# A recurrent and an attention layer on one core: the second half's attention input turned by transposing transfers

## The chip, the core and the metric

One core of one Trainium2 chip runs the whole program. Its engines are TensorE (PE in the profile; its weight loads are shown as PEld), VectorE (DVE), ScalarE (ACT), GpSimd (POOL) and SyncE (SP), which here only issues transfers. The metric is device time in microseconds (us) of one execution; lower is better.

## What is computed

Two layers on 256 tokens of width 1024, in fp32. Each layer is a feed-forward block, a mixer, and a second feed-forward block. The first layer's mixer is a gated linear recurrence, the second's is attention over keys and values that were computed from the first layer's output. The change lies at the entry to the second layer's attention and inside it. Cut to that, the reference is:

```python
f = swiglu(rms_norm(h, ffn1_pre_g[1]), ffn1_w_gate[1], ffn1_w_up[1], ffn1_w_down[1])
h = h + 0.5 * rms_norm(f, ffn1_post_g[1])
hn = rms_norm(h, mix_pre_g[1])
m = forgetting_attention(hn, attn_w_q[0], attn_w_o[0], k, v, c)
h = h + rms_norm(m, mix_post_g[1])

def forgetting_attention(xq, w_q, w_o, k, v, c):        # 16 heads of 64, blocks of 128 queries
    q = heads(xq @ w_q) * 64 ** -0.5
    for blk in range(2):
        logits = q[blk] @ k[:end].T + c[blk] - c[:end]  # end = 128, then 256; causal mask
        outs.append(softmax(logits) @ v[:end])
    return concat(outs) @ w_o
```

## The kernel before

**Tiles and halves.** The 256 tokens are two halves of 128 rows, t = 0 and t = 1. The residual `h[t]` is held with tokens in partitions. A product with a weight matrix needs its input turned, features in partitions; that turned input is the pair of tiles `xhi` and `xlo` with eight blocks k = 0 to 7 of 128 features each. Precision comes from a split: every weight and every input is written as an upper part (`hi`, a copy by ScalarE, L173 for weights) and the rest (`lo`, a difference by VectorE, L177), and a product is three matmuls: upper by upper, lower by upper, upper by lower.

**Units and slots.** The weights come in units of 512 KB (two blocks k by 512 columns for the q projection). A unit is loaded into one of 5 raw buffers by a transfer on SP's queue and split into one of 9 pairs of buffers. A slot is the work of one half on one unit, six large matmuls here (L454, L455, L458). `slot(t, i)` writes a slot's matmuls and ends with `tick()`. `prepare_next`, called by `tick`, loads and splits the next unit, as long as a unit of 9 places earlier is done in both halves; for the last four of W_o's eight units there is one more bound: unit i is not split before the first half has come to unit i - `near`, and `near = 3`.

**What sets the order.** TensorE's list is fixed by hand: it executes in the order in which the code was written. `defer(n, fn)` puts work off by n ticks, that is, by n slots. On the other engines a scheduler sets the order, in which work in `high_priority()` goes first and what is under `keep_in_program_order` keeps the order of writing. Each engine works through its list in that order, and an instruction that waits holds all behind it. The lists of SP and GpSimd include the transfers that they issue.

**The entry to attention.** `enter` ends a feed-forward block: it adds the normed output to `h[t]` (L298, L311) and puts off the making of the next input by `wait` = 3 slots. For attention, `inputs` does for each half: eight transposes on TensorE into two accumulators of tag `gt` (L226), a product with the gain on VectorE (L234), the upper part on ScalarE (L235), the rest on VectorE (L240). `stat` takes the sum of squares (L205) and two small GpSimd instructions (L198, L200) make the norm's factor from it, which is applied to q later. Elsewhere in the kernel the blocks k = 4 to 7 go another way (`by_transfer`): GpSimd copies the numbers into two planes of 16 bits (`planes`, L212), a transfer on SP's queue turns them (`swap`, L216), GpSimd puts the planes together (`join`, L220), and `turned_to_x` makes product, upper part and rest (L258, L259, L240).

**Attention.** For each half there are eight slots of q (two groups of 512 columns) and eight of W_o. When a group of q is complete, `heads_T` copies it to `htok` on VectorE (L1044). For t = 0 four transposes turn it (L1057, two slots later, copied to `qT` by ScalarE, L1059); for t = 1 the way over planes and a transfer is taken. Between the slots stand the small products of attention: `l` logits (L1194; then on VectorE the reduction with the bias, L1203, and on ScalarE eight exponentials, L1210), `n` the norming (L1217), `t` four transposes of probabilities (L1223, copied by ScalarE, L1225), and `v` the values (L1237). The string `ATT_ORDER` says in which order: a digit is a slot of that half, `l0` the next logits of the first half, and so on. The values gather in an accumulator of tag `mm` (four of these exist, two of each of the tags `gt` and `tr`):

```python
if hds[0] % 8 == 0:
    box["po"] = mmbank()
```

At the stage's begin `att_rows` loads the bias of the second half (2 MB) with a transfer on GpSimd's queue (L1038).

## Time and profile before

| what | value |
|---|---|
| median of three runs | 964.89 us (964.70 to 964.91) |
| profiled execution | 965.18 us, of which the span is 963.5 us |
| TensorE busy | 954.8 us, 99% |
| VectorE busy | 646.0 us, 67% |
| ScalarE busy | 527.5 us, 55% |
| GpSimd busy | 236.5 us, 25% |
| granted clock of TensorE | 0.999 |
| transfers | 199.84 MB, mean 207 GB/s |
| attention stage | from about 709 to 783 us of the span |

A row of the trace in order of time shows start, duration, engine, line, operation, `out<-in`, partitions by elements and type, and a count where several equal instructions are taken together; a bracket at its end gives the idle time before it and what ended that. Matmuls overlap their neighbours at start and end, so a difference of starts says what one costs, and not the duration. SPq and POOLq are the transfers that SP and GpSimd issue.

### The profile page before, as it was taken

To read this page: it belongs to the slowest core of one execution; us is meant where nothing else is said; L and a number is where in the kernel's file an instruction comes from. 1 tells how busy PE (TensorE), PEld (TensorE's weight loads), DVE (VectorE), ACT (ScalarE), POOL (GpSimd) and SP (SyncE) were. 2 spreads that over 40 slices of the span, in tenths; PEclk is the share of its full clock that TensorE was granted. 3 is DMA by queue.
4 is the path that set the end of the run, shared out by engine and by line. 5 is a ranking of instruction groups with operands and counts; after the bars stand their busy time and mean duration, and the time that the engine had idled before them with its cause. 6 is when DMAs were issued, how large, how long until landed. Compare 5 with 4: busy or idle time off the path is not lost.

```text
span 963.5 us, 12847 instructions
## 1 busy us (share of the span) xinstructions
PE 954.8 (99%) x4559; PEld 789.6 (82%) x4559; DVE 646.0 (67%) x845; ACT 527.5 (55%) x750; POOL 236.5 (25%) x229
## 2 busy tenths in 40 slices
PE   9999999999999999999999999999999999999997
PEld 6888888898878888888898888888887788888885
DVE  6758774578997756664686566665488876666642
ACT  7446454568986555444565445444366865444431
POOL 2812230130003323230023623224022133232200
PEclk9999999999999999999999999999999999999999
DMA  8788996485338687676559979879763478777731
GB/s 283 227 229 252 250 291 196 143 222 166 128 110 244 203 238 215 201 245 193 138 158 313 249 223 262 223 190 289 227 255 102 121 210 260 208 225 234 217 110 44
DMA packets 153158, 199.84 MB, mean 207 GB/s; under 512 B 71390, under 2 KB 90182, under 8 KB 152966
## 3 DMA queue, kind: packets, MB, share of 16 engines
q1 hardware_dynamic: 150406, 192.11, 67.4%
q0 software_dynamic: 2080, 6.38, 2.3%
q8 instruction: 36, 0.59, 0.2%
q10 hardware_dynamic: 608, 0.53, 0.2%
q14 instruction: 28, 0.23, 0.1%
HBM read 182.19 MB, written 3.16 MB: 192 GB/s over the span
## 4 chain that ended last, share of the span: by engine, by line
PE 95%; DVE 2%; ACT 1%; issue 1%; POOL 0%; DMA 0%; POOLq 0%; DVEq 0%; ACTq 0%
PE mm L454 16%; PE mm L455 16%; PE mm L458 16%; PE mm L183 13%; PE mm L185 13%; PE mm L184 13%; PE gt L824 2%; PE mm L1340 1%; PE mm L190 1%; PE mm L191 1%; PE mm L192 1%; ACT pe L1210 1%; PE gt L226 1%; PE tr L127 0%; DVE wlo L177 0%
## 5 line engine op out<-in xcount | busy, mean ns | idle before, releaser
L177 DVE TENSOR_TENSOR wlo<-raw,whi 128x1024 fp32r<-128x1024 f32 (+5 forms) x329 | 423.0, 1293 | 213.9 <-ACT whi L173 212.4
L173 ACT ACTIVATE whi<-raw 128x1024 fp32r<-128x1024 f32 (+5 forms) x329 | 341.6, 1045 | 295.8 <-PE mm L458 107.2
L454 PE MATMUL mm<-whi,xhi 128*128 128x512 f32 x656 | 256.7, 391 | 0.0
L455 PE MATMUL mm<-wlo,xhi 128*128 128x512 f32 x656 | 255.5, 389 | 0.0
L458 PE MATMUL mm<-whi,xlo 128*128 128x512 f32 x656 | 202.2, 389 | 0.0
L454 PEld LDWEIGHTS mm<-whi,xhi 128*128 128x128 f32 x656 | 123.2, 188 | 25.9 <-issue 0.7
L458 PEld LDWEIGHTS mm<-whi,xlo 128*128 128x128 f32 x656 | 123.1, 188 | 26.0 <-DVE xlo L240 0.2
L455 PEld LDWEIGHTS mm<-wlo,xhi 128*128 128x128 f32 x656 | 123.2, 188 | 25.3 <-DVE wlo L177 0.3
L183 PE MATMUL mm<-whi,hhi 128*128 128x512 f32 x352 | 137.2, 390 | 0.0
L185 PE MATMUL mm<-whi,hlo 128*128 128x512 f32 x352 | 137.0, 389 | 0.0
L184 PE MATMUL mm<-wlo,hhi 128*128 128x512 f32 x352 | 137.0, 389 | 0.0
L569 POOL COPY pl<-prod 128x1024 uint16<-128x1024 uint16 (+1 forms) x48 | 67.7, 1410 | 168.9 <-DMA prod<-pl 168.9
L556 POOL COPY pl<-prod 128x1024 uint16<-128x1024 uint16 (+1 forms) x48 | 70.1, 1460 | 141.8 <-DVE prod L553 74.4
L185 PEld LDWEIGHTS mm<-whi,hlo 128*128 128x128 f32 x352 | 66.1, 188 | 13.7
L183 PEld LDWEIGHTS mm<-whi,hhi 128*128 128x128 f32 x352 | 66.1, 188 | 13.7
L184 PEld LDWEIGHTS mm<-wlo,hhi 128*128 128x128 f32 x352 | 66.1, 188 | 13.6
L198 POOL TENSOR_SCALAR nv<-ss 128x1 f32<-128x1 f32 x22 | 11.4, 517 | 252.8 <-ACT junk L205 252.8
L553 DVE SCALAR_TENSOR_TENSOR prod<-mm,rstd,sil 128x512 f32<-128x512 f32 (+1 forms) x48 | 33.7, 703 | 29.1 <-PE mm L458 24.8
L544 ACT ACTIVATE sil<-mm,rstd 128x512 f32<-128x512 f32 (+1 forms) x48 | 31.1, 650 | 32.4 <-PE mm L458 24.8
L575 DVE TENSOR_TENSOR hlo<-pl,hhi 128x512 fp32r<-128x512 f32 (+1 forms) x48 | 41.2, 858 | 3.6 <-ACT hhi L574 3.6
L183 PE MATMUL mm<-whi,xhi 128*128 128x512 f32 (+1 forms) x112 | 42.8, 382 | 0.0
L185 PE MATMUL mm<-whi,xlo 128*128 128x512 f32 (+1 forms) x112 | 42.5, 379 | 0.0
(235 smaller groups left out, 1067.8 us busy)
## 6 DMA issues: line engine op xcount, KB each, us to landing
raw<-in_ffn_w_down_dram SPq DMA_DIRECT2D x88, 512.0 KB
raw<-in_ffn_w_up_dram SPq DMA_DIRECT2D x80, 512.0 KB
raw<-in_ffn_w_gate_dram SPq DMA_DIRECT2D x78, 512.0 KB
raw<-in_rg_w_in_dram SPq DMA_DIRECT2D x10, 504.0 KB
raw<-in_rg_w_out_dram SPq DMA_DIRECT2D x10, 504.0 KB
raw<-in_ffn_w_gate_dram SPq DMA_DIRECT2D x19, 256.0 KB
raw<-in_ffn_w_up_dram SPq DMA_DIRECT2D x16, 256.0 KB
raw<-in_rg_w_in_dram SPq DMA_DIRECT2D x8, 512.0 KB
```

Of the source, the lines that this page charges most:

```text
L173: up = nc.scalar.activation(hi[:parts, c:c + m], rawv[:, c:c + m], AF.Copy)
L177: nc.vector.tensor_tensor(lo[:parts, c:c + m], rawv[:, c:c + m], hi[:parts, c:c + m].bitcast(F32), ALU.subtract)
L183: nc.tensor.matmul(ps, xh, wh, start=first, stop=False)
L184: nc.tensor.matmul(ps, xh, wl, start=False, stop=False)
L185: nc.tensor.matmul(ps, xl, wh, start=False, stop=last)
L454: nc.tensor.matmul(ps, get_x(t, k)[0], u.hi[:, c], start=k == 0, stop=False)
L455: nc.tensor.matmul(ps, get_x(t, k)[0], u.lo[:, c], start=False, stop=False)
L458: nc.tensor.matmul(ps, get_x(t, k)[1], u.hi[:, c], start=False, stop=k == nk - 1)
L553: nc.vector.scalar_tensor_tensor(pr[:, :nn], ps, rs[t][:, 0:1], s, ALU.mult, ALU.mult)
L556: nc.gpsimd.tensor_copy(halves.rearrange("p (h f) -> p h f", h=2), pr[:, :nn].bitcast(U16).rearrange("p (f h) -> p h f", h=2))
L569: nc.gpsimd.tensor_copy(halves.rearrange("p (f h) -> p h f", h=2), turned.rearrange("p (h a) b -> p h (a b)", h=2))
L575: keep(nc.vector.tensor_tensor(lv, x, hv.bitcast(F32), ALU.subtract))
```

## The change

It has five parts.

1. For one place, the second half's input in front of attention (`whole`: the block before was a feed-forward block, there is one destination, and t = 1), all eight blocks k are now turned by transfers. `enter` copies both halves of `h[1]` to planes right behind the update of h. Three slots later `whole_inputs` issues the two transposing transfers, takes the sum of squares, and lets GpSimd join the planes. `turned_to_x`, which got an argument n for the group of blocks, follows for k = 0 to 3 after three more slots and for k = 4 to 7 after four. The eight transposes on TensorE, and the products, upper parts and rests that `inputs` made, are no longer there.
2. The load of the second half's bias is put off by seven slots.
3. `near` is 5 rather than 3, so the last four units of W_o may each be split two units earlier.
4. The second accumulator of the second half's values comes from tag `gt` rather than `mm`.
5. `ATT_ORDER` is another list. It has the same slots and the same small products; more of the latter stand beside each other.

```diff
-    def turned_to_x(v, dests, more):
+    def turned_to_x(v, dests, more, n=1):
...
-                g = gT[:, gi + 4:gi + 8].unsqueeze(2).to_broadcast([P, 4, P])
+                g = gT[:, gi + 4 * n:gi + 4 * n + 4].unsqueeze(2).to_broadcast([P, 4, P])
...
-                tc.keep_in_program_order(nc.scalar.activation(xh[:, 4:, :], xs[i], AF.Copy))
+                tc.keep_in_program_order(nc.scalar.activation(xh[:, 4 * n:4 * n + 4, :], xs[i], AF.Copy))
             for xg, dest in zip(xs, dests):
-                x_lower(xg, dest, 1)
+                x_lower(xg, dest, n)
...
         by_transfer = (spare or t == 1) and not (half and (len(dests) == 1 or t == 0)) and not normed
+        whole = half and len(dests) == 1 and t == 1 and not normed
+        if whole:
+            with tc.high_priority():
+                hp = [hpool.tile([P, 512], F32, tag="t1", name=nm("hp"), bufs=2) for _ in range(2)]
+                for n in range(2):
+                    planes(hp[n].bitcast(U16), h[t][:, n * 512:(n + 1) * 512])
...
+        def whole_inputs():
+            ht = [pools["a"].tile([P, 512], F32, tag="pT", name=nm("ht"), bufs=4).bitcast(U16) for _ in range(2)]
+            with tc.high_priority():
+                for n in range(2):
+                    swap(ht[n], hp[n].bitcast(U16))
+            stat(t)
+            with tc.high_priority():
+                for n in range(2):
+                    join(hp[n].bitcast(U16).rearrange("p (f h) -> p h f", h=2), ht[n])
+            for n in range(2):
+                defer(3 + n, lambda n=n: turned_to_x(hp[n], dests, None, n))
...
-            defer(wait, inputs)
+            defer(wait, whole_inputs if whole else inputs)
...
-    near = 3
+    near = 5
...
-        tc.keep_in_program_order(nc.gpsimd.dma_start(att["bias1"], kv["bias1"]))
+        defer(7, lambda: tc.keep_in_program_order(nc.gpsimd.dma_start(att["bias1"], kv["bias1"])))
...
-                box["po"] = mmbank()
+                box["po"] = mmbank() if t == 0 or hds[0] == 0 else gtbank()
...
-    ATT_ORDER = ("0 0 0 0 0 0 0 l0 0 1 n0 l0 1 1 t0 n0 1 l0 v0 1 t0 n0 l0 1 v0 n0 1 t0 l1 1 v0 t0 n1 l1 0 v0 "
+    ATT_ORDER = ("0 0 0 0 0 0 0 l0 0 1 n0 l0 1 1 n0 1 t0 t0 l0 1 n0 l0 1 n0 1 v0 v0 t0 1 l1 v0 t0 n1 l1 0 v0 n1 l1 0 t1 "
...
```

Lines behind the change stand lower by up to 18 in the changed kernel: the exponentials are L1228 there, the copies to qT L1077, the q slots L472, L473 and L476. The next pieces are the engines' lists, where `x4` means four of that kind in a row, and numbers behind a name count tiles.

GpSimd's list where attention begins, first before, then in the changed kernel; h_75 is the second half's residual, hp the planes, ht what the transfer turned, and nv and rstd belong to the norm's factor.

```order
L198 TENSOR_SCALAR nv_6329<-ss_6320 128x1
L200 TENSOR_TENSOR rstd_6331<-nv_6329,mhalf 128x1
L1038 DMA bias_6347<-bias1d 128x4096
L198 TENSOR_SCALAR nv_6394<-ss_6391 128x1
L200 TENSOR_TENSOR rstd_6396<-nv_6394,mhalf 128x1
L212 COPY pl_6538<-htok_6536 128x1024
L220 COPY qT_6346<-htok_6536 128x2x512
```

```order
L198 TENSOR_SCALAR nv_6329<-ss_6320 128x1
L200 TENSOR_TENSOR rstd_6331<-nv_6329,mhalf 128x1
L212 COPY hp_6335<-h_75 128x1024
L212 COPY hp_6336<-h_75 128x1024
L198 TENSOR_SCALAR nv_6383<-ss_6380 128x1
L200 TENSOR_TENSOR rstd_6385<-nv_6383,mhalf 128x1
L220 COPY hp_6335<-ht_6376 128x2x512
L220 COPY hp_6336<-ht_6377 128x2x512
L1056 DMA bias_6351<-bias1d 128x4096
L212 COPY pl_6529<-htok_6527 128x1024
```

Four copies are new, two in front of the small instructions of the second sum of squares and two behind them, and the bias's load has gone from the third place to behind the four.

ScalarE's list from the second half's sum of squares (L205) to the end of the first logits' exponentials, before and then changed; pe are exponentials, mx the negated maxima that they read, whi a weight unit's upper part, here of W_o, and xg or hp the second half's input.

```order
L205 ACTIVATE junk_6392,ss_6391<-h_75 128x1024
L235 ACTIVATE xhi<-xg_6383 128x4x128
L235 ACTIVATE xhi<-xg_6386 128x4x128
L1059 ACTIVATE qT_6345<-tr_6419 128x512
L1210 ACTIVATE pe_6443,sm_6441<-pe_6443,mx_6442 128x128 x4
L1210 ACTIVATE pe_6455,sm_6441<-pe_6455,mx_6454 128x128 x2
L1059 ACTIVATE qT_6345<-tr_6495 128x512
L1210 ACTIVATE pe_6455,sm_6441<-pe_6455,mx_6454 128x128 x2
L173 ACTIVATE whi_6483<-raw_6481 128x1024
```

```order
L205 ACTIVATE junk_6381,ss_6380<-h_75 128x1024
L1077 ACTIVATE qT_6349<-tr_6410 128x512
L259 ACTIVATE xhi<-hp_6335 128x4x128
L173 ACTIVATE whi_6481<-raw_6479 128x1024
L1228 ACTIVATE pe_6437,sm_6435<-pe_6437,mx_6436 128x128 x3
L1077 ACTIVATE qT_6349<-tr_6493 128x512
L1228 ACTIVATE pe_6437,sm_6435<-pe_6437,mx_6436 128x128
L1228 ACTIVATE pe_6449,sm_6435<-pe_6449,mx_6448 128x128 x4
L259 ACTIVATE xhi<-hp_6336 128x4x128
L173 ACTIVATE whi_6503<-raw_6501 128x1024
```

The two upper parts of the input stood together ahead of the first copy to qT; now the first stands behind that copy, and the second behind the last of the eight exponentials. The unit's upper part, which stood behind them all, is ahead of the exponentials.

VectorE's list in the same logits' reductions, before and changed; htok is the second group of q of the first half, and `ISA` is a reduction or the read of its result.

```order
L1203 ISA pe_6455,mx_6454<-gt_6432,bias_2952 128x128
L1203 ISA mx_6454 128x1
L1044 TENSOR_SCALAR htok_6472<-mm_6406,rstd_6270 128x512
L1208 TENSOR_TENSOR mx_6442<-mx_6442,cq_2947 128x4
L1203 ISA pe_6455,mx_6454<-gt_6431,bias_2952 128x128
L1203 ISA mx_6454 128x1
```

```order
L1221 ISA pe_6449,mx_6448<-gt_6426,bias_2952 128x128
L1221 ISA mx_6448 128x1
L1062 TENSOR_SCALAR htok_6466<-mm_6397,rstd_6270 128x512
L258 TENSOR_TENSOR hp_6336<-hp_6336,gT 128x512
L1226 TENSOR_TENSOR mx_6436<-mx_6436,cq_2947 128x4
L1221 ISA pe_6449,mx_6448<-gt_6425,bias_2952 128x128
L1221 ISA mx_6448 128x1
```

The product of the second part of the input (L258) now stands there, ahead of the small sum that makes the first exponentials' maxima.

More of the change, by code (lines that the diff above doesn't have):

```diff
@@ L1268, in trunk_kernel @@
               lambda t: None, last=True)
-    ATT_ORDER = ("0 0 0 0 0 0 0 l0 0 1 n0 l0 1 1 t0 n0 1 l0 v0 1 t0 n0 l0 1 v0 n0 1 t0 l1 1 v0 t0 n1 l1 0 v0 "
-                 "n1 l1 t1 0 n1 l1 t1 0 n1 l1 v1 v1 t1 0 n1 l1 t1 0 n1 l1 v1 v1 t1 0 n1 l1 t1 0 n1 v1 v1 0 t1 1 "
-                 "t1 v1 1 v1 1 1 1 1 1 1")
+    ATT_ORDER = ("0 0 0 0 0 0 0 l0 0 1 n0 l0 1 1 n0 1 t0 t0 l0 1 n0 l0 1 n0 1 v0 v0 t0 1 l1 v0 t0 n1 l1 0 v0 n1 l1 0 t1 "
+                 "n1 l1 t1 0 n1 l1 v1 v1 t1 0 n1 l1 t1 0 n1 l1 v1 v1 t1 0 n1 l1 t1 0 n1 v1 v1 0 t1 1 t1 v1 1 v1 1 1 1 1 1 1")
     def half(t, i):
```

## The prediction

> **What bounds the kernel now.** I read the page's line of busy engines first, then the windows over attention, then TensorE's rows there in order of time, and last what stands before those rows on the other engines.
>
> The first view is the page's part 1, the next one the windows of 20 us over attention (span, then busy time and instructions of PE, PEld, DVE, ACT and POOL, the granted clock, the DMA share and GB/s).
>
> ```profile
> PE 954.8 (99%) x4559; PEld 789.6 (82%) x4559; DVE 646.0 (67%) x845; ACT 527.5 (55%) x750; POOL 236.5 (25%) x229
> ```
> ```profile
> 700.00:720.00 20.00, 20.00 (x100) 16.67 (x98) 17.87 (x23) 14.75 (x22) 5.12 (x9) 1.00 0.67 249
> 720.00:740.00 20.00, 19.76 (x128) 14.97 (x126) 14.83 (x63) 11.73 (x40) 3.57 (x2) 1.00 0.48 159
> 740.00:760.00 20.00, 20.00 (x147) 15.12 (x148) 18.47 (x58) 15.71 (x40) 2.41 (x2) 1.00 0.37 95
> ```
>
> TensorE is busy 99% of the span, at full clock, and in these windows all but 0.24 us of 60. So the change gains only work or waits that it takes off TensorE's list, and loses every microsecond that it makes TensorE wait. VectorE has 17.87 and 18.47 of 20 us taken in two of the three windows: what is put in its way there shows.
>
> TensorE's own rows, in order of time (start, duration, line, names):
>
> ```profile
> 713.35 1.03 PE L226 MATMUL gt<-ident,h 128*128 128x128 f32 x8
> 714.14 0.48 PE L454 MATMUL mm<-whi,xhi 128*128 128x512 f32 x1
> 714.45 0.40 PE L455 MATMUL mm<-wlo,xhi 128*128 128x512 f32 x1
> 718.32 0.60 PE L1057 MATMUL tr<-ident,htok 128*128 128x128 f32 x4
> 722.83 0.40 PE L454 MATMUL mm<-whi,xhi 128*128 128x512 f32 x1
> 724.21 0.39 PE L454 MATMUL mm<-whi,xhi 128*128 128x512 f32 x1
> 725.58 0.60 PE L1057 MATMUL tr<-ident,htok 128*128 128x128 f32 x4
> 725.93 0.48 PE L454 MATMUL mm<-whi,xhi 128*128 128x512 f32 x1
> ```
>
> Here is the clock of the place. A slot (six large matmuls) takes 1.38 us (722.83 to 724.21). At 713.35 the eight transposes of the second half's h; at 718.32 and 725.58 the turns of the first half's q; at 722.83 the second half's first slot, at 725.93 its third, the first that reads the input's k = 4 to 7. I follow the change to these two slots.
>
> **The change part by part.**
>
> *The transposes go.* 713.35 to 714.14 is 0.79, and the matmul after them takes 0.31 instead of 0.23: 0.87 off TensorE. The q turn could then start at 717.45 instead of 718.32.
>
> *What comes instead* is two copies to planes and two back on GpSimd, two transposing transfers on SP's queue, and on VectorE and ScalarE a product, a copy and a difference per half. The product and the split replace as many of before, but stand elsewhere in their queues. VectorE in the trace of before:
>
> ```profile
> 711.51 1.41 DVE L311 SCALAR_TENSOR_TENSOR h<-t,rstd,h 128x512 f32<-128x512 f32 x2
> 712.84 2.35 DVE L177 TENSOR_TENSOR wlo<-raw,whi 128x1024 fp32r<-128x1024 f32 x2
> 721.44 0.29 DVE L1203 CUSTOM_DVE_ANT_0 pe<-gt,bias 128x128 f32<-128x128 f32 x1 [3.19 <-PE gt L1194]
> 721.66 0.08 DVE L1203 DVE_READ_ACCUMULATOR2_ANT mx<- 128x1 f32 x1
> 723.03 0.75 DVE L1044 TENSOR_SCALAR htok<-mm,rstd 128x512 f32<-128x512 f32 x1 [0.16 <-PE mm L458]
> ```
> ```profile
> 789.81 0.69 DVE L258 TENSOR_TENSOR hp<-hp,gT 128x512 f32<-128x512 f32 x1 [3.26 <-POOL hp L220]
> ```
>
> And the same copies of GpSimd, once with VectorE quiet and once beside two splits:
>
> ```profile
> 741.04 1.04 POOL L212 COPY pl<-htok 128x1024 uint16<-128x1024 uint16 x1 [3.74 <-DVE mx L1208]
> ```
> ```profile
> 781.51 1.97 POOL L212 COPY hp<-h 128x1024 uint16<-128x1024 uint16 x1 [1.51 <-DVE h L311]
> 788.43 1.34 POOL L220 COPY hp<-ht 128x1024 uint16<-128x1024 uint16 x1 [3.14 <-DMA ht<-hp]
> ```
> ```profile
> 781.36 3.19 DVE L177 TENSOR_TENSOR wlo<-raw,whi 128x1024 fp32r<-128x1024 f32 x2
> ```
>
> Alone the copy to planes takes 1.04. At 781.51 it takes 1.97, and the two splits under it 3.19 instead of 2.35 (712.84): the copy waited for the first split, the second split for the copy. The Trainium skill (SBUF — State Buffer, "Who interferes with whom") says why: a VectorE instruction with two SBUF inputs and a GpSimd instruction that reads SBUF exclude each other for the whole instruction. It adds that one with at most one SBUF input does not take part. This trace agrees with the first by 1.97 against 1.04. By the rule the sum is the one below, without it that of the first rival.
>
> In the changed kernel the two copies fall on the two splits at 712.84. The first half of h is there at 712.2; the copy waits for the second update and runs 712.9 to 713.9, a split to 715.05, the second copy to 716.05, the other split to 717.2 (before: 715.19), the q tile in 0.7 to 717.9. TensorE wanted it at 717.45: **a new wait of 0.5**. The second half's first slot then comes at 722.83 - 718.32 + 717.95 = 722.46.
>
> The transfers, and what waits for them:
>
> ```profile
> 732.50 1.25 SPq L216 DMA_TRANSPOSE htok<-pl  x1
> 783.51 1.25 SPq L216 DMA_TRANSPOSE ht<-hp  x1
> ```
> ```profile
> 735.62 1.68 POOL L220 COPY qT<-htok 128x1024 uint16<-128x1024 uint16 x1 [3.15 <-DMA htok<-pl]
> ```
>
> From the issue to the copy back it was 3.12 (732.50 to 735.62) and 4.92 (783.51 to 788.43, with other loads in the queue). From 713.95 and 716.1 that is 717.1 and 719.2 at best. GpSimd has its two small rstd instructions behind the last split, to 718.0, so the copies back (1.34 each) run to 719.35 and 720.7. The product of the first part (0.69) meets the second copy back and ends at 721.35, its xhi at 722.05, its xlo at 722.75: in time for the slot at 722.46, whose xlo products come 0.9 later. Late landing moves this by 0.2 only, since the product then goes ahead of the second copy.
>
> *The second part is the one that costs.* On VectorE it stands in the middle of the first logits' reductions, on ScalarE behind all eight exponentials of those logits. From 722.75: six reductions at 0.22 (721.44 to 721.66), the other q tile (0.7), the product (0.65) and two small sums: the first maxima are ready at 725.45. ScalarE's rows of before give the rest:
>
> ```profile
> 724.29 0.39 ACT L1210 ACTIVATE pe<-pe,mx 128x128 f32<-128x128 f32 x1
> 724.67 0.39 ACT L1210 ACTIVATE pe<-pe,mx 128x128 f32<-128x128 f32 x1
> 726.22 0.60 ACT L1059 ACTIVATE qT<-tr 128x512 f32<-128x512 f32 x1
> 726.71 0.39 ACT L1210 ACTIVATE pe<-pe,mx 128x128 f32<-128x128 f32 x1
> 727.48 1.04 ACT L173 ACTIVATE whi<-raw 128x1024 fp32r<-128x1024 f32 x1
> 728.42 0.58 ACT L1225 ACTIVATE pT<-tr 128x512 f32<-128x512 f32 x1
> ```
> ```profile
> 776.80 0.64 ACT L259 ACTIVATE xhi<-qT 128x512 fp32r<-128x512 f32 x1 [0.25 <-DVE qT L258]
> ```
>
> An exponential with its sum takes 0.38, the copy to qT 0.49, a W_o upper part 0.94, xhi 0.64. ScalarE's W_o upper part now stands ahead of the exponentials and waits for the second half's first slot, whose weight buffer it takes: 722.46 + 1.38 + 0.2 = 724.05, so it is through at 725.0, before the maxima. Then 725.45 + 8 x 0.38 + 0.49 + 0.64 = 729.6, and about 0.1 for the semaphores and starts: 729.7. TensorE has done two slots and the q turn (0.36) at 722.46 + 2.76 + 0.36 = 725.58, and its next row is the third slot, which reads that part. **A wait of 4.1.** Nothing behind it can pass: TensorE's list is fixed.
>
> *Fewer stretches.* What a stretch of small products costs beside itself:
>
> ```profile
> 733.87 0.62 PE L458 MATMUL mm<-whi,xlo 128*128 128x512 f32 x2
> 734.42 0.66 PE L1237 MATMUL mm<-pT,v 128*64 128x128 f32 x8
> 735.01 0.50 PE L454 MATMUL mm<-whi,xhi 128*128 128x512 f32 x1
> 735.35 0.39 PE L455 MATMUL mm<-wlo,xhi 128*128 128x512 f32 x1
> ```
> ```profile
> 737.35 0.73 PEld L1194 LDWEIGHTS gt<-kT,qT 64*128 64x128 f32 x8 [0.48 <-POOL qT L220]
> ```
>
> After two matmuls (0.45) from 733.87 the values start 0.10 late, and the matmul after them takes 0.34 instead of 0.23: 0.21 for a stretch that holds products of 64 rows or columns. Transposes alone cost that only at their end (0.08, above), and four of them start 0.08 earlier than eight do by half, so merging those is worth nothing. The list has one stretch of the dear kind less: -0.21. The wait of 0.48 for the second half's qT at 737.35 goes but for the 0.10 of any start, since on TensorE's list another slot (1.38) now stands ahead of it: -0.38. Together **-0.6**; between 0 and -0.8.
>
> *W_o five ahead and the output bank.* Two waits of before can go:
>
> ```profile
> 760.62 0.65 PE L1237 MATMUL mm<-pT,v 128*64 128x128 f32 x7 [0.16 <-ACT pT L1225]
> ```
> ```profile
> PEld mm L183 <- DVE t L298: 0.5, 1, 0.5
> ```
>
> The first is 0.16, for probabilities that were copied too late. The second is up to 0.5, for an accumulator whose bank the first half still held; the values' second bank now comes from another tag, so an accumulator is free. Against them, VectorE's last weight split now stands between a reciprocal and the product that a later turn waits for: 1.2 (half of 2.35), of which slots ahead of the turn hide the larger part; I count 0.4. **Net 0**; from -0.4 to +1.2. The W_o transfers themselves are issued in front of and behind the two transposing ones on SP's queue, long before their splits, and stay hidden.
>
> *The bias* is fetched behind GpSimd's copies back, at 720.7 instead of 711.49:
>
> ```profile
> bias<-bias1d POOLq DMA_DIRECT2D x1, 2048.0 KB, 11.8
> ```
>
> It lands near 733, before the second half's first logits (737.35 before, later now): nothing.
>
> **Sum**: -0.87 + 0.5 + 4.1 - 0.6 + 0 = +3.1. The profiled execution took 965.18 (span 963.5), 0.29 above the median of 964.89; I take the sum to the median: **968.0 us**. 0.2% of it is 1.93 us, about what a measurement of this kernel can tell from no change.
>
> **The rivals.**
>
> *The copies do not block the splits.* Then no q turn waits (0 for 0.5), the first xlo is ready at 721.4, the maxima at 724.1, ScalarE's W_o part at 724.5 (slot at 721.96) decides, xhi is there at 728.75 and TensorE waits from 725.08: 3.65. The sum is -0.87 + 3.65 - 0.6 = +2.2: 967.1. For it speaks that GpSimd could lose each race at 712.9; against it the rows at 781.
>
> *More waits behind it.* The second half's q goes through the same GpSimd copies, 1.2 us are open in the last two turns, and a transfer that takes 4.92 instead of 3.12 uses up the 1.4 that the first logits of the second half have to spare. With +1.2 and 0.4 of that: 969.6.
>
> *No wait at the third slot: it gets faster.* If the second xhi were there at 725.6, the sum would be -0.87 - 0.6 - 0.4 = -1.9: 963.0. The exponentials would have to start by 721.3; but their logits leave TensorE no sooner than 720.5, and their reductions take over 2 us on VectorE even alone. It decides at that point and no other, and only with an order on ScalarE that is not the one listed. The Trainium skill (Perfetto Trace Analysis, "Identifying the Most-Contended Engine") says to work on the engine with the highest occupancy first; that is TensorE here, and the change takes work off it. By that rule this rival would be the likeliest; the busy line agrees on which engine it is, and only the order of ScalarE's rows speaks against it.
>
> **How the numbers follow.** Around 968.0 (967.6 to 968.9) 0.50; copies that do not block (966.3 to 967.6) 0.25; more waits (above 968.9) 0.15; little or no wait (below 966.3) 0.10, of which 0.03 are below 962.96. 966.82 is the bound for slower: from the second case 0.16 lie above it. Slower 0.81, same 0.16, faster 0.03. The range 965.4 to 969.8 leaves out most of the last case and the end of the third, about 0.15.
>
> **What would show it.** TensorE: no L226 in front of attention's first slots; the first q turn under 0.5 later than the slot before it ends, and a wait of some 4 us before the third slot of the second half, put down to ScalarE's xhi (L259) or the exponentials. GpSimd: four copies between 712 and 721, those to planes near 1.9 rather than 1.04, and VectorE's two splits at 3.2 or more. The wait for qT before the second half's first logits gone. I am wrong if TensorE runs through that place with less than 2 us of waiting, if the transfers land so late that the first slot of the second half waits too, or if the waits are in the last turns rather than there.

## The result

The changed kernel takes **970.69 us** (median of six runs, 969.88 to 972.91), the kernel before 964.87 in runs beside it (964.32 to 964.91): a ratio of 1.0063, with a 95% interval from 1.0053 to 1.0074. It is slower by 5.8 us, and the forecast was slower by 3.1, with 969.8 as the range's upper end. The sign and the place came out as forecast; the size did not.

The first view is again the busy engines of the page's part 1, now of the changed kernel; the second its windows of 20 us, with the same columns as before.

```profile
PE 957.2 (99%) x4551; PEld 791.5 (82%) x4551; DVE 645.2 (66%) x845; ACT 527.5 (54%) x750; POOL 242.4 (25%) x233
```
```profile
700.00:720.00 20.00, 19.99 (x95) 16.41 (x94) 17.57 (x20) 14.14 (x22) 8.78 (x11) 1.00 0.66 190
720.00:740.00 20.00, 15.86 (x86) 12.29 (x85) 15.01 (x41) 9.99 (x26) 3.60 (x4) 0.83 0.70 238
740.00:760.00 20.00, 19.54 (x140) 14.55 (x139) 15.88 (x61) 14.20 (x43) 3.74 (x3) 1.00 0.31 74
```

TensorE executes 8 instructions fewer and is busy 2.4 us longer (957.2 after 954.8). The second window tells why: it stands idle for 4.14 of 20 us, and **the granted clock, 1.00 in every window of attention before, is 0.83**. I had counted the first and had no term for the second.

TensorE's rows in order of time, at the places that the prediction named:

```profile
718.73 0.66 PE L1075 MATMUL tr<-ident,htok 128*128 128x128 f32 x4
726.10 0.60 PE L1075 MATMUL tr<-ident,htok 128*128 128x128 f32 x4
730.83 0.79 PE L472 MATMUL mm<-whi,xhi 128*128 128x512 f32 x1 [4.14 <-ACT xhi L259]
733.56 0.63 PE L472 MATMUL mm<-whi,xhi 128*128 128x512 f32 x1
736.12 1.12 PE L1241 MATMUL tr<-ident,pe 128*128 128x128 f32 x8
737.16 1.16 PE L1212 MATMUL gt<-kT,qT 64*128 64x128 f32 x16
753.39 0.63 PE L1241 MATMUL tr<-ident,pe 128*128 128x128 f32 x4 [0.46 <-DVE pe L1235]
763.84 0.63 PE L1241 MATMUL tr<-ident,pe 128*128 128x128 f32 x4 [0.45 <-DVE mx L1226]
766.02 0.63 PE L1241 MATMUL tr<-ident,pe 128*128 128x128 f32 x4 [0.17 <-ACT pe L1228]
```

The profiled execution, 972.91, is the slowest of the six, and 1.14 us of it came in before this stage (its first transposes of the first half's h start at 704.06 rather than at 702.92). They came in at the kernel's start, which the change does not touch: at 8.35 a matmul of 512 columns still takes 0.63 us there, and before it took 0.40 from 7.15 on. So I measure from the stage's start. From these transposes to the next ones, behind W_o, it was 68.14 us before and is 74.42 now (771.06 and 778.48 are their starts): +6.28 in this stage, the one that the change touches. Its parts, each as a distance from the stage's start against the same distance before:

| | before | after | step |
|---|---|---|---|
| first q turn | 15.40 | 14.67 | -0.73: eight transposes less (-0.87) and 0.14 of waiting |
| second half's third slot | 23.01 | 26.77 | +4.38: 22.39 would be due, 0.35 behind the second q turn (726.10) |
| the two slots 3 and 4 | 2.76 | 5.29 | +2.53: 730.83 to 736.12, at half clock |
| eight transposes | 0.79 | 1.04 | +0.25: the first of them at half clock |
| the rest of the stage | | | -0.15: what the list saves, against three new waits (0.46, 0.45, 0.17) and 0.11 lost between the first q turn and the third slot |

Why the third slot waits can be read from ScalarE's rows and from VectorE's and GpSimd's in front of them:

```profile
722.53 0.64 ACT L259 ACTIVATE xhi<-hp 128x512 fp32r<-128x512 f32 x1 [2.46 <-DVE hp L258]
724.91 1.06 ACT L173 ACTIVATE whi<-raw 128x1024 fp32r<-128x1024 f32 x1 [1.74 <-PE mm L476]
726.60 0.40 ACT L1228 ACTIVATE pe<-pe,mx 128x128 f32<-128x128 f32 x1 [0.63 <-DVE mx L1226]
729.78 0.39 ACT L1228 ACTIVATE pe<-pe,mx 128x128 f32<-128x128 f32 x1
730.17 0.61 ACT L259 ACTIVATE xhi<-hp 128x512 fp32r<-128x512 f32 x1
```
```profile
713.98 4.04 DVE L177 TENSOR_TENSOR wlo<-raw,whi 128x1024 fp32r<-128x1024 f32 x2
720.80 1.70 DVE L258 TENSOR_TENSOR hp<-hp,gT 128x512 f32<-128x512 f32 x1 [2.12 <-POOL hp L220]
723.81 0.28 DVE L1221 CUSTOM_DVE_ANT_0 pe<-gt,bias 128x128 f32<-128x128 f32 x1
725.81 0.68 DVE L258 TENSOR_TENSOR hp<-hp,gT 128x512 f32<-128x512 f32 x1
```
```profile
713.47 3.47 POOL L212 COPY hp<-h 128x1024 uint16<-128x1024 uint16 x2 [0.85 <-DVE h L311]
719.42 2.58 POOL L220 COPY hp<-ht 128x1024 uint16<-128x1024 uint16 x2 [0.68 <-DMA ht<-hp]
```

It is the chain that the prediction wrote down: the copies to planes and the two splits shut each other out (3.47 for two copies and 4.04 for two splits, where the splits alone took 2.35), the product behind the copies back (1.70 rather than 0.69), the W_o part waiting for the first slot (724.91), the eight exponentials, and at 730.17 the second part's xhi. The profile puts the wait at 4.14; the prediction had 4.1.

What was not written down follows it. The next windows are cut to where the clock changes:

```profile
729.40:729.50 0.10, 0.00 (x0) 0.00 (x0) 0.10 (x1) 0.10 (x3) 0.00 (x0) 0.76 0.01 0
731.00:732.00 1.00, 1.00 (x3) 0.81 (x4) 1.00 (x3) 0.73 (x1) 0.00 (x0) 0.50 0.49 197
736.20:736.30 0.10, 0.10 (x2) 0.10 (x1) 0.00 (x0) 0.00 (x0) 0.00 (x0) 0.61 0.01 0
```

2.75 us after TensorE fell idle (its last transposes end at 726.70) the clock goes from 1.00 to 0.50, in the middle of the first of these windows, and it comes back in the middle of the last: 6.83 us at half clock. 1.4 us of that TensorE was waiting anyway; in the other 5.4 it did the work of 2.7.

### The profile page after: what moved, and what is told of

The parts are those of the page before. It is cut to its first block, busy times and chain, and to the rows that moved or that the text cites. A ratio compares the mean times of both kernels' runs of the same rounds, so it can differ in the third digit from the quotient of the medians.

```text
span 971.1 us, 12838 instructions
## 1 busy us (share of the span) xinstructions
PE 957.2 (99%) x4551; PEld 791.5 (82%) x4551; DVE 645.2 (66%) x845; ACT 527.5 (54%) x750; POOL 242.4 (25%) x233
## 4 chain that ended last, share of the span: by engine, by line
PE 92%; DVE 3%; ACT 2%; issue 2%; DMA 1%; POOL 1%; POOLq 0%; ACTq 0%; DVEq 0%
PE mm L472 16%; PE mm L473 16%; PE mm L476 16%; PE mm L183 13%; PE mm L185 12%; PE mm L184 12%; PE gt L842 2%; PE mm L1357 1%; ACT pe L1228 1%; PE mm L190 1%; PE mm L191 1%; PE mm L192 1%; DVE wlo L177 1%; DVE pe L1221 1%; DMA ht<-hp 0%
## 5 line engine op out<-in xcount | busy, mean ns | idle before, releaser
L472 PE MATMUL mm<-whi,xhi 128*128 128x512 f32 x656 | 257.4, 392 | 4.1 <-ACT xhi L259 4.1
L473 PE MATMUL mm<-wlo,xhi 128*128 128x512 f32 x656 | 256.4, 391 | 0.0
L476 PE MATMUL mm<-whi,xlo 128*128 128x512 f32 x656 | 203.0, 391 | 0.0
L472 PEld LDWEIGHTS mm<-whi,xhi 128*128 128x128 f32 x656 | 123.7, 189 | 30.2 <-ACT xhi L259 4.6
L476 PEld LDWEIGHTS mm<-whi,xlo 128*128 128x128 f32 x656 | 123.6, 189 | 26.2 <-DVE xlo L240 0.2
L473 PEld LDWEIGHTS mm<-wlo,xhi 128*128 128x128 f32 x656 | 123.8, 189 | 25.6 <-DVE wlo L177 0.3
```

The source lines that it names most:

```text
L472: nc.tensor.matmul(ps, get_x(t, k)[0], u.hi[:, c], start=k == 0, stop=False)
L473: nc.tensor.matmul(ps, get_x(t, k)[0], u.lo[:, c], start=False, stop=False)
L476: nc.tensor.matmul(ps, get_x(t, k)[1], u.hi[:, c], start=False, stop=k == nk - 1)
```

## The experiments

The theory at the start: the change loses by ScalarE's order at the third slot, once as a wait of 4.4 and once as the clock that the wait costs; the list, the W_o units and the bank are worth about nothing. The rivals: the later turns' waits carry the loss; the list does; or the transfers are late with any order. All kernels were timed in five or more runs beside runs of the kernel before on the same chip. Its medians there were 964.62, 964.69, 964.81 and 964.55.

### Filling the wait (e1_filled, e5_fill6)

```diff
+            if c == "1" and nxt[1] == n_ffn3 + 2:
+                keep_busy(17)
             half(int(c), nxt[int(c)])
```

`keep_busy(n)` writes n matmuls of a constant into a free accumulator that nobody reads. The other kernel has 6 in place of 17.

> The changed kernel, with 17 useless matmuls of 512 columns on constants (0.22 us each at full clock, 3.7 us) on TensorE ahead of the second half's third slot, where it waits for ScalarE. All other engines' lists are the same, so that slot starts when it did. Theory: the wait costs twice, once as waiting (4.4 us) and once because the granted clock falls to 0.5 while TensorE idles and stays there for some 6 us after it (2.5 to 2.8 us). With TensorE kept at work the clock stays at 1.00 and the time is 968.0, 2.7 less than the changed kernel's 970.7; the runs also lie closer together. Rival: the fall of the clock is a mark of the record and costs little, and the rest of the 5.8 us lies in the later turns (three new waits of 0.46, 0.46 and 0.17): then it stays at 970.5 or comes out slower.

Measured: **969.08** (968.17 to 969.57), ratio 1.0044 (1.0030 to 1.0058). TensorE's third slot and the windows, first of this kernel, then of the one with six:

```profile
729.18 0.50 PE L472 MATMUL mm<-whi,xhi 128*128 128x512 f32 x1 [0.40 <-ACT xhi L259]
```
```profile
720.00:740.00 20.00, 19.54 (x116) 14.01 (x114) 15.89 (x58) 13.39 (x42) 3.47 (x4) 1.00 0.73 232
```

It starts 26.88 from the stage's start (702.30), as late as without the filling, and yet the time is less: TensorE works through the wait, the clock stays at 1.00, and doing useless work saves 1.6 us of the median (1.4 if each is set against its own runs of the kernel before). The stage itself is 72.50 long, 1.9 less than in the changed kernel's profile. I had expected 2.7. Part of it is given back: with faster slots in front, a later turn of probabilities waits 0.81 where it waited 0.46.

> The changed kernel, with 6 useless matmuls (1.3 us) ahead of the third slot in place of 17, so that some 2.8 us of waiting stay. In the changed kernel's profile the granted clock fell 2.6 us after TensorE fell idle, and in the run with the earlier second part it fell behind a wait of 1.94 us. Theory: what counts is how much of some window of time TensorE stands idle, wherever that window happens to lie; so 2.8 us are still enough in part of the executions, and these spread from 968.5 (clock kept) to 971 (lost). Rival: it takes a wait of more than 3 us; then all lie at 968.2 to 969.6 as with 17. Second rival: any wait of 2 us does it, and the median stays at 970.7.

Measured: 970.35, and the six runs lie in two groups: 968.28 and 968.53, and 970.29, 970.40, 970.96 and 973.25. The records' mean clock is 0.998 in the first two and 0.995 to 0.997 in the others. The profiled run is of the first kind:

```profile
728.32 0.50 PE L472 MATMUL mm<-whi,xhi 128*128 128x512 f32 x1 [2.12 <-ACT xhi L259]
```
```profile
720.00:740.00 20.00, 17.83 (x109) 13.71 (x107) 16.02 (x57) 13.51 (x42) 4.06 (x4) 1.00 0.76 245
```

Here 2.12 us of waiting have left the clock at 1.00. They were to be 2.8. In this execution the transfers had landed before GpSimd was ready for them, 3.71 after their issue at 713.27 (4.43 in the changed kernel, with 0.68 of waiting), and the first exponentials start 0.78 earlier from the stage's start than in the changed kernel's profile:

```profile
716.98 3.28 POOL L220 COPY hp<-ht 128x1024 uint16<-128x1024 uint16 x2
```

So a wait of 2 to 3 us seems to lose the clock in some executions and not in others: "any wait of 2 us does it" falls by the profile, "it takes more than 3 us" by the four slower runs, as far as their mean clock can tell. Whether these waited longer than 2.12 or only at another moment is not shown, since only one of the six was traced.

### Half of the change at a time (e3_list, e4_whole, e8_list_near3)

e4_whole has the old `ATT_ORDER`, `near = 3` and the old bank. e3_list has the rest of the change without the transfers; e8_list_near3 is e3_list with three units ahead:

```diff
-        whole = half and len(dests) == 1 and t == 1 and not normed
+        whole = False
...
-    near = 5
+    near = 3
```

> The kernel before with the first half of the change alone: the turned input by transfers and the bias's load put off, with the old list, three units ahead and the old output bank. ScalarE's list has the same order up to the second upper part. Theory: -0.9 for the transposes, +0.1 for the q turn, +4.4 waiting and +2.7 lost clock: 971.2 (970 to 973). Rival: the wait comes only with the new list: 965 or less.

Measured: 969.84 (969.31 to 970.70), ratio 1.0054 (1.0042 to 1.0067), a little under what was expected. The wait is there without the new list, and the clock fell for 6.83 us here too:

```profile
728.90 0.80 PE L472 MATMUL mm<-whi,xhi 128*128 128x512 f32 x1 [4.15 <-ACT xhi L259]
```
```profile
727.70:727.80 0.10, 0.00 (x0) 0.00 (x0) 0.02 (x1) 0.10 (x2) 0.00 (x0) 0.69 0.00 0
734.50:734.60 0.10, 0.10 (x2) 0.02 (x1) 0.00 (x0) 0.00 (x0) 0.00 (x0) 0.68 0.00 0
```

> The kernel before with the second half of the change alone: the merged list, W_o up to five units ahead, the output bank from the other tag, the bias's load put off. The eight transposes stay. Theory: these parts are worth about nothing together, as the sum of the profiled execution says (the stretches saved are eaten by three new waits of 0.46, 0.46 and 0.17 in front of turns): 964.3 to 965.3. Rival: they cost a good part of the 5.8 us: 967 or more. Second rival, the list was worth 0.6 to 1.0 and its waits came from the late entry: 963.9.

Measured: 965.82 (965.24 to 967.74), ratio 1.0014 (1.0005 to 1.0023). This is more than the theory had. TensorE waits for a product of VectorE that stands behind two W_o splits and behind a small sum that takes 1.15 (beside a copy back of GpSimd from 734.82 to 736.14), where the same takes 0.15 in the changed kernel, at 726.41:

```profile
736.85 0.63 PE L1241 MATMUL tr<-ident,pe 128*128 128x128 f32 x4 [1.42 <-DVE pe L1235]
```
```profile
732.52 1.22 DVE L177 TENSOR_TENSOR wlo<-raw,whi 128x1024 fp32r<-128x1024 f32 x1
733.73 1.22 DVE L177 TENSOR_TENSOR wlo<-raw,whi 128x1024 fp32r<-128x1024 f32 x1
734.96 1.15 DVE L1226 TENSOR_TENSOR mx<-mx,cq 128x4 f32<-128x4 f32 x1
736.03 0.68 DVE L1235 TENSOR_TENSOR pe<-pe,sm 128x512 f32<-128x512 f32 x1
```

> The merged list and the other bank, with the transposes of before and W_o three units ahead. With five units ahead there was a wait of 1.42 for VectorE's product of the probabilities at 736.85, and the time was 965.82, 1.2 more than before. Theory: the W_o splits in front of that product make this wait; three units ahead it goes: 964.0 to 964.6. Rival: the merged turns make it, since both turns now stand behind one slot: 965.5 or more.

Measured: 964.59 (964.15 to 965.17), ratio 0.9998 (0.9989 to 1.0006): the wait is gone, and no wait on TensorE in its attention stage is above 0.54. With one of the two splits gone from there, the small sum takes 0.13, ahead of GpSimd's copy, and the product starts at 734.44. The difference between the two, 1.2 us, is the price of splitting W_o two units earlier in this kernel, which keeps the transposes. The merged list with the other bank, and the bias's load put off, are together worth nothing that could be measured.

### Another order on ScalarE (e2_early, e6_early_old, e7_early_near3)

```diff
-                defer(3 + n, lambda n=n: turned_to_x(hp[n], dests, None, n))
+                defer(3, lambda n=n: turned_to_x(hp[n], dests, None, n))
```

Both parts of the input are then written ahead of the first logits, and on ScalarE both upper parts stand ahead of the exponentials. e6 is this edit on e4_whole, e7 has three units ahead besides.

> The changed kernel, with the second part of the turned input put off by three slots like the first, rather than four. On ScalarE its upper part then stands behind the first part's, ahead of all exponentials. Theory: the wait at the third slot was ScalarE's order alone. Both it (4.4) and the lost clock (2.7) go, and 970.7 becomes 963.6 to 964.3, somewhat below the kernel before. Rival: GpSimd's copies and the transfers are what is late, so that a wait of 2 us or more stays at the first or third slot: 966 or more. Second rival: VectorE now makes both products ahead of the first reductions, and the first turn of probabilities waits instead for 1 to 2 us: 965 to 966.

Measured: **968.16** (967.89 to 970.89), ratio 1.0044 (1.0032 to 1.0057). The wait at the third slot is gone, and the time is not. It went to three later turns:

```profile
725.07 0.66 PE L1075 MATMUL tr<-ident,htok 128*128 128x128 f32 x4 [0.76 <-DVE htok L1062]
730.15 0.63 PE L1241 MATMUL tr<-ident,pe 128*128 128x128 f32 x4 [1.22 <-ACT whi L173]
739.14 1.04 PE L1241 MATMUL tr<-ident,pe 128*128 128x128 f32 x4 [1.93 <-DVE pe L1235]
```
```profile
739.20:739.30 0.10, 0.10 (x1) 0.10 (x2) 0.00 (x0) 0.10 (x1) 0.00 (x0) 0.53 1.05 410
742.60:742.70 0.10, 0.10 (x3) 0.03 (x2) 0.00 (x0) 0.00 (x0) 0.00 (x0) 0.91 0.00 0
```

After the last of them the clock fell again, for 3.41 us, when TensorE was already back at work. The second rival was the right one, and too small. This profiled execution took 969.38; the three runs from 967.89 to 968.16 have a mean clock of 0.998 or 0.999 rather than 0.997 and probably did not lose it, so that the lost clock is hardly in the median.

> Only the first half of the change (old list, three units ahead, old bank), with both parts of the turned input put off by three slots. With the new list this order left waits of 0.77 at the second q turn, 1.22 and 1.94 at later turns. Theory: the entry itself is late by the lock between GpSimd's copies and VectorE's two-input instructions, the first exponentials start 1 to 2 us later for it, and the first turn of probabilities waits for them with any list: -0.9 + 0.1 + 0.8 + 1 to 1.5, no lost clock: 965.6 to 966.2. Rival: those waits came from the merged list and the early W_o units; then they are gone and it is 964.0 to 964.6.

Measured: 966.91 (966.12 to 967.41), ratio 1.0022 (1.0013 to 1.0030), with waits of 1.00 at the second q turn, 1.03 at the first probabilities and 0.59 for the second half's q. So the entry is late with any list, by more than the theory had.

> The changed kernel with both parts of the input put off by three slots, and W_o three units ahead rather than five. Theory: the wait of 1.94 at 739 came from the two W_o splits that VectorE has ahead of the probabilities' product there; without them it goes, and its lost clock (about 1.4) too: 968.2 becomes 964.8 to 965.6. Rival: VectorE is late there for the whole entry, and it stays above 967.

Measured: 967.08 (966.44 to 967.65), ratio 1.0023 (1.0014 to 1.0033). The wait of 1.93 is gone with the two units, as the theory said, but only 1.1 us with it, since 0.68 and 1.25 at the two turns stay, and the lost clock was hardly in the median of e2. The time is the rival's.

### What makes the entry late (e9_act_planes to e12_held)

In e9 ScalarE makes the planes, in e12 W_o's last loads keep their written order on SP's queue besides:

```diff
-                    planes(hp[n].bitcast(U16), h[t][:, n * 512:(n + 1) * 512])
+                    nc.scalar.activation(hp[n].bitcast(U16).rearrange("p (h f) -> p h f", h=2), ..., AF.Copy)
...
-            nc.sync.dma_start(v, src)
+            (tc.keep_in_program_order if keep else lambda x: x)(nc.sync.dma_start(v, src))
```

> The run with both parts put off by three slots and W_o three ahead (967.08), with the two copies to planes made by ScalarE (which stood idle for 4.2 us there) rather than GpSimd. Theory: GpSimd's copies and VectorE's two weight splits shut each other out (the splits take 4.04 for two rather than 2.35, the copies 3.47 for two rather than 2.08), and what is late for it are the second q turn (0.68) and the first probabilities (1.25). Without these two copies the splits take 2.4 again, the copies back start about 1 us earlier, and 1 to 1.7 us of the waits go: 965.4 to 966.1. Rival: the waits come from the transfers, which are as late with any engine: 967 or more. Second rival: ScalarE's W_o part, which now stands ahead of the exponentials and waits for the second half's first slot, gives a new wait: 967 to 968.

Measured: **971.12** (970.87 to 972.54), ratio 1.0069 (1.0056 to 1.0082). The theory falls. The first rival says only that the transfers are as late as before, and they are later; the second's W_o part comes long after the wait that counts. VectorE, SP, GpSimd and TensorE in order:

```profile
712.08 2.35 DVE L177 TENSOR_TENSOR wlo<-raw,whi 128x1024 fp32r<-128x1024 f32 x2
```
```profile
713.36 0.33 SPq L164 DMA_DIRECT2D raw<-in_attn_w_o_dram  x1
713.78 4.09 SPq L216 DMA_TRANSPOSE ht<-hp  x2
```
```profile
720.61 2.56 POOL L220 COPY hp<-ht 128x1024 uint16<-128x1024 uint16 x2 [4.58 <-DMA ht<-hp]
```
```profile
724.38 0.80 PE L473 MATMUL mm<-whi,xhi 128*128 128x512 f32 x1 [3.04 <-ACT xhi L259]
```

The lock is out of the way: two splits take 2.35 again. But a raw buffer is free earlier by that, and a load of 512 KB goes out ahead of the transposing transfers. The copies back start 6.83 after their issue (4.43 in the changed kernel, 714.99 to 719.42), and now the second half's *first* slot waits, 3.04. The clock falls for it at 723.72 and is back at 730.55, and two later turns of probabilities wait 1.31 and 1.19. That the load ahead is what made the transfers late is argued here, not shown; the next run holds it back.

> The run with the planes on ScalarE (971.12), with one thing more: the loads of W_o's last four units keep the order of writing on SP's queue, so that none is issued ahead of the two transposing transfers. In that run a 512 KB load went out 0.4 us ahead of them, since VectorE's faster splits had freed its raw buffer, and it took 6.8 us from the issue of the transfers to the copy back, where it had been 4.05 with no load ahead. Theory: that load made the 3.04 us of waiting and the lost clock. Without it the copy back starts near 717.5, no slot waits, the first exponentials start 1 to 2 us earlier than with GpSimd's planes, and the time is 963.8 to 965.2; the units loaded later (behind the transfers of q) are needed only some 10 us after that. Rival: the transfers are slow beside any load in flight (four W_o loads were issued before them), and it stays at 966.5 or more. Second rival: the late loads of W_o are themselves waited for in the last slots: 965.5 to 967.

Measured: 966.83 (965.96 to 968.37), ratio 1.0024 (1.0013 to 1.0034). That is 4.3 us less than e9, by the load held back and by the order of ScalarE, which came out with it: the W_o part is behind the exponentials here. How much is whose these two kernels don't tell. And the entry is still late:

```profile
712.89 3.39 SPq L216 DMA_TRANSPOSE ht<-hp  x2
```
```profile
719.16 2.58 POOL L220 COPY hp<-ht 128x1024 uint16<-128x1024 uint16 x2 [3.35 <-DMA ht<-hp]
```
```profile
722.95 0.50 PE L473 MATMUL mm<-whi,xhi 128*128 128x512 f32 x1 [1.82 <-ACT xhi L259]
```
```profile
723.90:724.00 0.10, 0.10 (x3) 0.06 (x2) 0.10 (x1) 0.00 (x0) 0.00 (x0) 0.84 0.71 164
727.30:727.40 0.10, 0.10 (x2) 0.01 (x1) 0.10 (x2) 0.04 (x1) 0.00 (x0) 0.59 1.15 492
```

With no such load the copies back still start 6.27 after the issue in this execution. It is the second slowest of its eight runs (968.32), and its clock fell, for 3.41 us, after a wait of 1.82. Why the transfers took so long here is open; four W_o loads and a gain had been issued ahead of them, as in every kernel of this family.

The last two turn only k = 4 to 7 by a transfer, as the kernel does elsewhere, e10 with the merged list, e11 with the old list and bank; in both `whole` is False and `near` is 3. The line that they share:

```diff
-        by_transfer = (spare or t == 1) and not (half and (len(dests) == 1 or t == 0)) and not normed
+        by_transfer = (spare or t == 1) and not (half and t == 0) and not normed
```

> The merged list, the other bank and W_o three ahead (964.59), with the blocks k = 4 to 7 alone of the second half's input turned by a transfer, as the kernel does it elsewhere, and k = 0 to 3 by four transposes. Theory: four transposes fewer are worth 0.44 at most; with one copy each way on GpSimd the lock delays one split (1 us) and nothing on TensorE waits for that, and the second part's upper part stands ahead of the exponentials on ScalarE: 964.0 to 964.5. Rival: the first logits' reductions come late by the product and copy that now stand in front of them, and the first turns wait for 0.5 to 1: 964.8 to 965.3.

> The kernel before (old list, old bank, three ahead), with the blocks k = 4 to 7 alone of the second half's input turned by a transfer and the bias's load put off. Theory as for the other list, with less room behind the first logits: 964.2 to 964.9. Rival: the first turn of probabilities, one slot earlier in this list, waits for 0.5 to 1.0: 965.0 to 965.5.

Measured: 966.11 (965.11 to 967.38) and 966.50 (966.00 to 967.07), ratios 1.0014 (1.0005 to 1.0023) and 1.0017 (1.0008 to 1.0026). Both are slower than their rivals said. In e10 one turn of probabilities waits 0.95, as its rival had it; in e11 the first turn waits 0.30, less than its rival's 0.5, and the values wait 0.31 and the second half's logits 0.48 for their q.

One distance tells how late the entry is: from the stage's start to the first exponential of the first logits. The first line is of the kernel before, the second of e10:

```profile
723.88 0.41 ACT L1210 ACTIVATE pe<-pe,mx 128x128 f32<-128x128 f32 x1 [4.28 <-DVE mx L1208]
```
```profile
724.83 0.40 ACT L1228 ACTIVATE pe<-pe,mx 128x128 f32<-128x128 f32 x1 [2.83 <-DVE mx L1226]
```

It is 20.96 before, in e3 and in e8, 21.76 in e5, 21.79 in e11, 22.54 in the changed kernel, 22.60 to 22.76 in e4, e1 and e10, 23.12 to 23.60 in e7, e2 and e6, 25.42 in e12 and 26.42 in e9. The input's product stands ahead of the first logits' reductions on VectorE, and it waits for GpSimd's copy back. With transposes it waits for nothing there. Four or eight transposes are worth 0.44 or 0.87 us, and every kernel in which a transfer stands in for them starts its exponentials 0.8 us later or more. It does not order those kernels by time: e12, at 25.42, takes 966.83, and the changed kernel, at 22.54, takes 970.69, since its wait is behind the exponentials. That the late exponentials are what e10 and e11 lose by is argued from their waits and not shown by itself. None of these kernels beats the one before.

## Why the prediction was right and wrong

**Right, with the size:** the transposes (-0.87, and the first q turn came 0.73 earlier with 0.14 of waiting); the wait at the third slot (4.1 forecast, 4.14 in the profile), its cause on ScalarE and its chain (e2_early took that wait away by the order alone); the copies that block the splits, so that the rival "the copies do not block" is out: the row of 1.97 was the right one to go by, and the Trainium skill's rule (SBUF — State Buffer, "Who interferes with whom"), which it was set beside, holds in this trace by 4.04 against 2.35. The same section of the Trainium skill excepts the 2-port perf modes from its rule on one SBUF input, which the prediction left out; no term rests on it.

Two small readings were off. The first maxima at 725.45 leave 0.03 for "two small sums" that take 0.07 each (723.70 to 723.77). And "late landing moves this by 0.2 only, since the product then goes ahead" came out the other way round: in e5, where the transfers landed early, the product went ahead (0.69) and the first xhi started 16.74 from the stage's start; in the changed kernel they landed late, the product met the second copy back (1.70), and xhi started at 18.47.

**Wrong, and the step that failed:** the price of the wait. The prediction said that the change "loses every microsecond that it makes TensorE wait", and the sum counted the wait at its length, 4.1, and nothing for the work behind it, which so stayed at 1.38 a slot. The two slots behind the wait took 5.29 together, since the granted clock had fallen to 0.50, and the transposes behind them 0.25 more: a term of +2.8 in the profiled execution that the sum did not have. Filling the wait with useless matmuls showed it apart from the wait: 1.6 us of the median, with 0.35 of that term given back at a later turn; where the rest of the difference lies is open, but the profiled execution is also the slowest of the six. The other terms were off by +0.28 (the third slot's delay, 4.38 for 4.1), -0.36 (the q turn) and +0.45 (list, W_o and bank, -0.15 for -0.6), which nearly cancel, by luck. The trace of before had rows for the lost clock that the prediction did not use, windows at its end, where TensorE has run out of work (span, busy times, clock, DMA share, GB/s):

```profile
957.00:958.00 1.00, 0.12 (x1) 0.00 (x0) 0.06 (x1) 0.69 (x2) 0.00 (x0) 1.00 0.00 0
962.00:963.00 1.00, 0.00 (x0) 0.00 (x0) 0.00 (x0) 0.00 (x0) 0.00 (x0) 0.71 0.00 0
```

The last matmul ends at 957.12, and the clock falls 5.3 us later. By that row alone a wait of 4.1 could have been taken for safe, but its price was open: nothing in it said how short a lag can be.

The Trainium skill (TensorE: Matmul & The Clock Gate, "What's actually happening") states the rule: the clock is halved after a window of 3.4 us without work and given back after one with work. The prediction did not draw on this rule, which would have put a price on a long wait. The half clock's lengths here, 6.83, 6.83, 6.83, 3.41 and 3.41 us, are one or two of these windows. But a window without any work is not what it took here: 1.82 and 1.93 us of waiting in one window were enough. 1.42 in one window was not, and neither was e5's 2.12, which fell on two windows, 1.43 in one and 0.69 in the next (the last section has the windows).

**Mis-sized:** *W_o five ahead* was taken at 0 between -0.4 and +1.2; it is +1.2 (965.82 against 964.59) in the kernel with the transposes, the upper end: one split more (1.22) stands ahead of the product that a turn waits for, and by it the small sum behind it meets GpSimd's copy (1.15 rather than 0.13). In the changed kernel, where the list, W_o and the bank come to -0.15 together, its part was not measured. *Fewer stretches* was taken at -0.6; with the bank and the bias's load it is -0.1 at the median, and zero is within its interval (the stage of e8 in its one profiled execution is 67.76 long, 0.38 less than before). *The q turn* was taken at +0.5 and cost 0.14.

**The rivals.** "More waits behind it" was right that they come (0.46, 0.45 and 0.17), and had 969.6, nearest to the measured time, but by luck: with all that the list saves, the rest of the stage came to -0.15, and what was missing is the clock's. "No wait at the third slot: it gets faster" is out twice: the wait was there, and where e2_early took it away, other turns waited instead. Its condition, "an order on ScalarE that is not the one listed", was not enough.

## What to carry to other kernels

A wait of about 2 us or more on a TensorE that is otherwise always at work can be priced twice: its length, and, where the clock falls for it, up to half of the next 3.4 or 6.8 us (2.8 here). Where work is taken off the fullest engine and given to a chain of three others, compare when the *next* consumer starts, here the first exponentials, and not only whether the moved result is in time. An engine that is made faster frees its buffers earlier, and the next load can then go out ahead of a transfer somebody waits for (713.36 and 713.78 in e9).

## What the runs showed of the hardware

The granted clock of TensorE was 1.00 or 0.50, and it changed at steps of 3.413 us that run through the whole execution: in the changed kernel's trace it is at 1.00 for 720.21 us, at 0.50 for 6.83 and at 1.00 for 232.11, which are 211, 2 and 68 of these steps, and in the other thirteen traces the lengths between two changes are whole numbers of steps too, to 0.01. Cut at these steps, the windows show how much idle time it took. In the step before each fall inside attention TensorE stood idle for 1.82 (e12), 1.93 (e2), 2.38 (e9), 2.75 (the changed kernel) and 2.98 us (e4). Steps with 1.42 (e3), 1.48 (e5) or less kept it. The bound between is not sharp: at the end of the kernel before, a step with 1.89 us idle (955.60 to 959.01) kept it, and the next one, wholly idle, lost it.

It stayed at 0.50 for one step, 3.41 us, where TensorE worked all through that step (e2, e12), and for two, 6.83 us, where the wait still took 0.65 to 1.38 us of the first (e9, e4, the changed kernel). In e2 it fell at 739.2, although TensorE had been back at work since 739.14.

So one program can differ from run to run by where its wait lies among these steps: the runs of e5 lay at 968.3 to 968.5 and at 970.3 to 973.3, and six runs of the changed kernel spread over 3.0 us where those of before spread over 0.6. It is not the only cause of a spread: the start of the kernel gave 1.14 us in one execution, and the landing of the transfers moved the entry by 0.78.
